# Mean over rows: the last group of rows loaded as 4, 4, 2 and 1 blocks, with five small stores

## The chip, the core and the metric

The kernel runs on one core of a Trainium2 chip. The metric is the device time of one execution in microseconds (us); before the change the median of three runs is 628.7 us (628.64 to 629.09). The profile's span, from the first to the last instruction, is 626.7 us in the profiled execution.

Engines go by these names: PE is TensorE (matmuls), with its weight loads as PEld; DVE is VectorE; ACT is ScalarE; POOL is GpSimd; SP is SyncE, which does no arithmetic here and issues transfers. SBUF is the on-chip memory of 128 partitions; PSUM is where TensorE's sums go.

## What is computed

```python
def setup_inputs():
    return {"x": np.random.randn(8192, 8192).astype(np.float32)}

def reference(x):
    return np.mean(x, axis=0)
```

x has 8192 rows and 8192 columns of 4 bytes, 268.4 MB, and each element is used once. The kernel takes the rows in 64 groups of 128, one row to a partition. Groups are added element by element into an accumulator `acc` of 128 x 8192, and at the end TensorE sums over the 128 partitions: a matmul with a stationary matrix filled with 1/8192 gives the mean of each column. The columns are counted in 16 blocks of F = 512.

## The kernel before

The buffers: four row buffers of 128 x 8192 that are loaded in turn, a fifth one `both` for the sum of a pair, and `acc`. PSUM holds three banks for blocks 0 to 11 and two ends for blocks 12 to 15.

```python
    F = 512
    W = F // 2
    WHOLE = 12
    G = M // P                     # 64 groups
    ...
    both = bufs[:, U - 2, :]
    acc = bufs[:, U - 1, :]
    ones = sb.tile([P, 32], f32, name="ones")
    ahead = sb.tile([P, 4 * F], f32, name="ahead")
    tail = sb.tile([P, W], f32, name="tail")
    ...
    banks = [psp.tile([P, F], f32, name=f"bank{b}") for b in range(3)]
    ends = [psp.tile([P, W], f32, name=f"end{e}") for e in range(2)]
```

All loads are issued by SyncE in program order. A load waits, through the buffer, for the VectorE add that last read it. VectorE's adds wait by way of a no-op on ScalarE or GpSimd, which gathers two waits into one. `landed` is a no-op on SyncE that waits for given transfers.

Three blocks of group 60 (`head`) and four blocks of group 63 (`ahead`) are loaded at the start, so that the last group has less to load. From group 6 to 53 the rows come in pairs: the two of a pair are added into `both`, and `both` into `acc`. From group 54 on they come one by one.

```python
    load(head[:], rows(G - 4)[:, :3 * F])
    first, second = load_rows(0, 0, 4), load_rows(4, 4, 2)
    load(ahead[:], rows(G - 1)[:, 8 * F:WHOLE * F])
    ...
    while g < G - 10:
        u = (g + 2) % 4
        dma = load_rows(g, u, 2)
        add(both, bufs[:, u, :], bufs[:, u + 1, :], [dma])
        add(acc, acc, both, [])
        g += 2

    while g < G - 4:
        row = bufs[:, (g + 2) % 4, :]
        add(acc, acc, row, [load(row, rows(g))])
        g += 1
    for lo, loaded in [(3, 3), (5, 0)]:               # groups 60 and 61
        row = bufs[:, (g + 2) % 4, :]
        dma = load(row[:, loaded * F:], rows(g)[:, loaded * F:])
        add(acc[:, lo * F:], acc[:, lo * F:], row[:, lo * F:], [dma])
        g += 1
    r61, r62, r63 = [bufs[:, (g + 1 + j) % 4, :] for j in range(3)]
    load(r62, rows(g))
    tc.keep_in_program_order(nc.gpsimd.tensor_add(
        out=acc[:, 13 * F:], in0=acc[:, 13 * F:], in1=r62[:, 13 * F:]))
    g += 1
    for lo, hi in [(0, 8), (12, 14), (14, 16)]:
        load(r63[:, lo * F:hi * F], rows(g)[:, lo * F:hi * F])
```

What VectorE and GpSimd do not add (parts of groups 60 to 63) goes to TensorE directly, in the order of a plan; the matmuls of one column add up in PSUM. A matmul uses a quarter of the array's columns (`tile_position`), so that four run side by side. Blocks 12 to 15 are cut in halves of 256 columns.

```python
    plan = [
        (ahead, 8, 12), (acc, 3, 5), (acc, 0, 3), (r61, 0, 5), (head, 0, 3),
        (acc, 5, 12), (r62, 0, 12), (r62, 12, 13), (acc, 12, 14), (acc, 14, 16),
        (r63, 0, 8), (r63, 12, 14), (r63, 14, 16),
    ]
    ...
        tc.keep_in_program_order(nc.tensor.matmul(
            out=dst[32 * q:32 * q + 32, :],
            lhsT=ones[:],
            rhs=cols,
            ...
            tile_position=(0, 32 * q),
        ))
```

Last come the copies out of PSUM and the stores. Four stores are made, two issued by ScalarE and two by SyncE.

```python
    copy(res[:, 2, :], banks[2][:])
    s2 = store(nc.scalar, out[8 * F:12 * F].rearrange("(q c) -> q c", q=4), res[0:P:32, 2, :],
               loads[-3])
    for b in range(2):
        copy(res[:, b, :], banks[b][:])
    copy(tails[0], ends[0][:])
    nc.vector.tensor_copy(out=tails[1], in_=ends[1][:])
    landed(*loads[-8:-6])
    landed(*loads[-6:-4])
    landed(*loads[-4:-2])
    landed(*joins.values())
    s01 = store(nc.sync, out[:8 * F].rearrange("(b q c) -> q b c", b=2, q=4), res[0:P:32, 0:2, :])
    s3 = store(nc.scalar, *end(0))
    store(nc.sync, *end(1))
    landed(loads[-2], s2)
    landed(loads[-1], adds[-1])
    landed(s01, s3)
    hold = tc.keep_in_program_order(nc.vector.nop()).ins
    tc.add_manual_dep(hold, s01.name, sync, reason="VectorE ends late")
```

## Time and profile before

| quantity | value |
|---|---|
| time, median of 3 | 628.7 us |
| span of the profiled execution | 626.7 us |
| VectorE busy | 526.1 us (84%), 60 instructions |
| TensorE busy | 17.6 us (3%), 124 matmuls |
| GpSimd busy | 4.0 us (1%) |
| ScalarE busy | 3.5 us (1%) |
| read from device memory | 268.44 MB, 428 GB/s over the span |
| first VectorE add starts | 43.77 us |
| GpSimd's add of 1536 columns | 615.74, for 3.47 us |
| last load's signal | 623.02 us |

The page of the profile cuts the span into 40 equal slices and gives, for each, the busy share of an engine in tenths, and of the 16 transfer engines as the row DMA. A group of instructions is one line: source line, engine, operation, output<-input with shapes, count, then total busy time and mean duration in ns, then the idle time ahead of it and what ended most of it. The chain of work that ended last is followed back from the last instruction; each piece gives its start, its length and what it was. In a timeline, SPq and ACTq are the queues on which SyncE and ScalarE issue transfers; the time of such an issue is not the time of the transfer.

### The profile page before, as it was taken

What the parts mean: (1) busy time and instruction counts of PE and PEld (TensorE: products, weight loads), DVE (VectorE), ACT (ScalarE), POOL (GpSimd) and SP (SyncE); (2) the same over time, 40 slices, a digit from 0 to 9 for tenths busy, and PEclk for the clock granted to TensorE, in tenths of its full rate; (3) what the DMA queues carried; (4) which work ended last, traced back from release to release, by engine and by line L of the source; (5) the groups of instructions that cost most, each with busy time, mean ns of one, the idle gap of its engine ahead of it and who ended that gap; (6) DMA issues with size and microseconds to landing.
All of it is one profiled execution on the core that took longest, in us unless ns stands there. A gap on an engine that the chain in (4) does not pass through costs nothing.

```text
span 626.7 us, 475 instructions
## 1 busy us (share of the span) xinstructions
PE 17.6 (3%) x124; PEld 5.1 (1%) x124; DVE 526.1 (84%) x60; ACT 3.5 (1%) x6; POOL 4.0 (1%) x7
## 2 busy tenths in 40 slices
PE   0000100000000000000000000000000000000027
PEld 0000000000000000000000000000000000000002
DVE  0028999999888998888988889888898888999991
ACT  0000000000000000000000000000000000000001
POOL 0000000000000000000000000000000000000002
PEclk9999999999999999999999999999999999999999
DMA  9999999999999999999999999999999999999997
GB/s 385 468 402 409 461 443 427 410 460 406 464 402 468 402 468 402 468 402 468 402 468 402 468 402 468 402 460 410 443 427 414 456 402 435 435 435 435 420 433 305
DMA packets 5926, 268.50 MB, mean 428 GB/s; under 512 B 656, under 2 KB 664, under 8 KB 1060
## 3 DMA queue, kind: packets, MB, share of 16 engines
q1 hardware_dynamic: 5908, 268.46, 99.2%
q8 instruction: 1, 0.02, 0.0%
q10 hardware_dynamic: 16, 0.01, 0.0%
q14 instruction: 1, 0.01, 0.0%
HBM read 268.44 MB, written 0.03 MB: 428 GB/s over the span
## 4 chain that ended last, share of the span: by engine, by line
DMA 56%; DVE 33%; another core or an unknown queue 10%; issue 0%; SPq 0%; PE 0%; ACTq 0%; POOLq 0%; POOL 0%
DMA bufs<-in_x_dram 56%; DVE bufs L95 33%; SPq L75 0%; PE end L169 0%; ACTq L98 0%; DVE tail L201 0%; POOLq L98 0%; POOL ready L62 0%; POOL ones L59 0%; POOLq L228 0%
## 5 line engine op out<-in xcount | busy, mean ns | idle before, releaser
L95 DVE TENSOR_TENSOR bufs<-bufs 128x8192 f32<-128x8192 f32 (+3 forms) x59 | 525.6, 8909 | 87.9 <-DMA bufs<-in_x_dram 43.8
L169 PE MATMUL bank<-bufs,ones 128*32 128x512 f32 x74 | 12.8, 709 | 540.4 <-DVE bufs L95 539.9
L201 DVE COPY tail<-end 128x256 f32<-128x256 f32 x1 | 0.4, 425 | 10.2 <-PE end L169 10.2
L169 PEld LDWEIGHTS bank<-bufs,ones 128*32 128x32 f32 x74 | 3.2, 120 | 549.5 <-DVE bufs L95 541.6
L136 POOL TENSOR_TENSOR bufs<-bufs 128x1536 f32<-128x1536 f32 x1 | 3.5, 3469 | 614.6 <-DMA bufs<-in_x_dram 614.6
L183 ACT COPY bufs<-bank 128x512 f32<-128x512 f32 x3 | 1.8, 586 | 619.2 <-PE bank L169 616.6
L169 PE MATMUL bank<-ahead,ones 128*32 128x512 f32 x8 | 1.9, 1058 | 65.7 <-DMA ahead<-in_x_dram 65.7
L169 PE MATMUL end<-bufs,ones 128*32 128x256 f32 x36 | 3.3, 384 | 0.1
L169 PE MATMUL bank<-head,ones 128*32 128x512 f32 x6 | 1.9, 600 | 0.0
L169 PEld LDWEIGHTS end<-bufs,ones 128*32 128x32 f32 x36 | 1.4, 109 | 2.4 <-DMA bufs<-in_x_dram 0.9
L116 ACT ACT_TABLE_LOAD x1 | 1.3, 1283 | 0.7 <-PEq L228 0.7
L169 PEld LDWEIGHTS bank<-ahead,ones 128*32 128x32 f32 x8 | 0.2, 140 | 65.6 <-issue 65.6
L183 ACT COPY bufs<-end 128x256 f32<-128x256 f32 x1 | 0.4, 378 | 0.0
L169 PEld LDWEIGHTS bank<-head,ones 128*32 128x32 f32 x6 | 0.4, 108 | 0.6 <-issue 0.6
L116 ACT COPY warm<-ones 128x32 f32<-128x32 f32 x1 | 0.2, 218 | 0.0
L62 POOL TENSOR_TENSOR ready<-ones 128x1 f32<-128x1 f32 x1 | 0.2, 193 | 0.1
L59 POOL MEMSET ones<- 128x32 f32 x1 | 0.1, 125 | 0.3 <-POOLq L228 0.3
L228 POOL MEMSET const-bfloat16-1.0<- 128x1 bf16 x1 | 0.1, 101 | 0.0
L228 POOL MEMSET const-uint8-127<- 128x1 uint8 x1 | 0.1, 101 | 0.0
L228 POOL MEMSET const-float32-0.0<- 128x1 f32 x1 | 0.1, 99 | 0.2 <-issue 0.2
L228 POOL MEMSET const-float32-1.0<- 128x1 f32 x1 | 0.1, 99 | 0.0
## 6 DMA issues: line engine op xcount, KB each, us to landing
bufs<-in_x_dram SPq DMA_DIRECT2D x8, 4096.0 KB, 24.1
bufs<-in_x_dram SPq DMA_DIRECT2D x1, 3328.0 KB
bufs<-in_x_dram SPq DMA_DIRECT2D x1, 2048.0 KB, 20.2
ahead<-in_x_dram SPq DMA_DIRECT2D x1, 1024.0 KB
bufs<-in_x_dram SPq DMA_DIRECT2D x2, 512.0 KB, 21.5
head<-in_x_dram SPq DMA_DIRECT2D x1, 768.0 KB
bufs<-in_x_dram SPq DMA_DIRECT2D x26, 29.9
out_dram<-bufs ACTq DMA_DIRECT2D x1, 8.0 KB
```

The costliest lines, as they stand in the source:

```text
L59: nc.gpsimd.memset(ones[:], 1.0 / M)
L62: nc.gpsimd.tensor_add(out=ready[:], in0=ones[:, 0:1], in1=ones[:, 1:2]))
L95: ins = nc.vector.tensor_add(out=dst, in0=a, in1=b).ins
L116: tc.keep_in_program_order(nc.scalar.copy(out=warm[:], in_=ones[:]))
L136: tc.keep_in_program_order(nc.gpsimd.tensor_add(out=acc[:, 13 * F:], in0=acc[:, 13 * F:], in1=r62[:, 13 * F:]))
L169: tc.keep_in_program_order(nc.tensor.matmul(out=dst[32 * q:32 * q + 32, :], lhsT=ones[:], rhs=cols, start=all(d is not dst or k != q for d ...
L183: tc.keep_in_program_order(nc.scalar.copy(out=dst, in_=src))
L201: nc.vector.tensor_copy(out=tails[1], in_=ends[1][:])
L228: nc = _bacc.Bacc("TRN2", target_bir_lowering=False, num_devices=1)
```

## The change

The end is rearranged. Early on, two blocks of group 60 (14 and 15) and five of group 63 (9 to 13) are loaded instead of three and four, into one buffer `early`. The five of group 63 are added to `acc` by GpSimd in the middle of the run, behind groups 24 and 32, so that TensorE no longer takes any early block. VectorE adds blocks 0 to 13 of group 60 and blocks 3 to 13 of group 61; GpSimd adds blocks 14 and 15 of group 61 behind VectorE's last add, then 14 and 15, and 8, of group 62. TensorE takes three blocks of group 61 instead of five.

The late part of group 63 is 11 blocks instead of 12, as blocks 4 to 7, 0 to 3, 14 and 15, and 8. The five blocks 9 to 13 have all their sums before group 63 comes and are stored early as `wide`. Blocks 14 and 15 (`two`) are cut in quarters of 256 columns, block 8 (`last`) in quarters of 128, so that the last load is followed by four matmuls of 128 columns and a copy of 128 columns. There are five stores instead of four. It is meant to leave less to load, add, copy and store behind the last transfer.

```diff
--- before.py
+++ after.py
@@ -40,8 +40,7 @@
     M, N = x.shape
     P = nc.NUM_PARTITIONS
     F = 512
-    W = F // 2
-    WHOLE = 12
+    W = F // 4
     G = M // P
     U = 6
     sync = mybir.DependencyInfo(mybir.DependencyClass.Sync, mybir.DependencyReason.DATA)
@@ -53,15 +52,17 @@
     both = bufs[:, U - 2, :]
     acc = bufs[:, U - 1, :]
     ones = sb.tile([P, 32], f32, name="ones")
-    ahead = sb.tile([P, 4 * F], f32, name="ahead")
+    early = sb.tile([P, 7 * F], f32, name="early")
     tail = sb.tile([P, W], f32, name="tail")
     warm = sb.tile([P, 32], f32, name="warm")
     nc.gpsimd.memset(ones[:], 1.0 / M)
     ready = sb.tile([P, 1], f32, name="ready")
     tc.keep_in_program_order(
         nc.gpsimd.tensor_add(out=ready[:], in0=ones[:, 0:1], in1=ones[:, 1:2]))
-    banks = [psp.tile([P, F], f32, name=f"bank{b}") for b in range(3)]
-    ends = [psp.tile([P, W], f32, name=f"end{e}") for e in range(2)]
+    banks = [psp.tile([P, F], f32, name=f"bank{b}") for b in range(2)]
+    wide = psp.tile([P, 2 * F], f32, name="wide")
+    two = psp.tile([P, 2 * W], f32, name="two")
+    last = psp.tile([P, W], f32, name="last")
 
     loads = []
 
@@ -103,81 +104,97 @@
             tc.add_manual_dep(ins, nop.name, sync, reason="waits for both at once")
         elif adds:
             tc.declare_no_dep(ins, group="loads", reason="the add ahead waited")
+        tc.declare_no_dep(ins, group="early", reason="the no-op waited, or the add behind it")
         tc.add_to_no_dep_group("adds", ins)
         adds.append(ins)
 
-    head = sb.tile([P, 3 * F], f32, name="head")
-    load(head[:], rows(G - 4)[:, :3 * F])
+    load(early[:, 5 * F:], rows(G - 4)[:, 14 * F:])
     first, second = load_rows(0, 0, 4), load_rows(4, 4, 2)
-    load(ahead[:], rows(G - 1)[:, 8 * F:WHOLE * F])
+    load(early[:, :5 * F], rows(G - 1)[:, 9 * F:14 * F])
     add(bufs[:, 2:4, :], bufs[:, 2:4, :], bufs[:, 0:2, :], [first])
     add(bufs[:, 4:6, :], bufs[:, 4:6, :], bufs[:, 2:4, :], [second])
     add(acc, acc, both, [])
     tc.keep_in_program_order(nc.scalar.copy(out=warm[:], in_=ones[:]))
+    ahead = []
     g = 6
     while g < G - 10:
         u = (g + 2) % 4
         dma = load_rows(g, u, 2)
         add(both, bufs[:, u, :], bufs[:, u + 1, :], [dma])
-        add(acc, acc, both, [])
+        add(acc, acc, both, ahead)
+        ahead = []
+        if g in (24, 32):
+            lo, hi = (0, 4) if g == 24 else (4, 7)
+            cols = slice((9 + lo) * F, (9 + hi) * F)
+            ins = tc.keep_in_program_order(nc.gpsimd.tensor_add(
+                out=acc[:, cols], in0=acc[:, cols], in1=early[:, lo * F:hi * F])).ins
+            tc.add_to_no_dep_group("early", ins)
+            ahead = [ins]
         g += 2
 
     while g < G - 4:
         row = bufs[:, (g + 2) % 4, :]
         add(acc, acc, row, [load(row, rows(g))])
         g += 1
-    for lo, loaded in [(3, 3), (5, 0)]:
+    for lo, hi, loaded in [(0, 14, 14), (3, 14, 16)]:
         row = bufs[:, (g + 2) % 4, :]
-        dma = load(row[:, loaded * F:], rows(g)[:, loaded * F:])
-        add(acc[:, lo * F:], acc[:, lo * F:], row[:, lo * F:], [dma])
+        dma = load(row[:, :loaded * F], rows(g)[:, :loaded * F])
+        cols = slice(lo * F, hi * F)
+        add(acc[:, cols], acc[:, cols], row[:, cols], [dma])
         g += 1
     r61, r62, r63 = [bufs[:, (g + 1 + j) % 4, :] for j in range(3)]
     load(r62, rows(g))
-    tc.keep_in_program_order(nc.gpsimd.tensor_add(
-        out=acc[:, 13 * F:], in0=acc[:, 13 * F:], in1=r62[:, 13 * F:]))
+    for row, lo, hi in [(r61, 14, 16), (r62, 14, 16), (r62, 8, 9)]:
+        cols = slice(lo * F, hi * F)
+        ins = tc.keep_in_program_order(nc.gpsimd.tensor_add(
+            out=acc[:, cols], in0=acc[:, cols], in1=row[:, cols])).ins
+        if row is r61:
+            tc.add_manual_dep(ins, adds[-1].name, sync, reason="VectorE goes first")
     g += 1
-    for lo, hi in [(0, 8), (12, 14), (14, 16)]:
+    for lo, hi in [(4, 8), (0, 4), (14, 16), (8, 9)]:
         load(r63[:, lo * F:hi * F], rows(g)[:, lo * F:hi * F])
 
-    plan = [
-        (ahead, 8, 12),
-        (acc, 3, 5),
-        (acc, 0, 3),
-        (r61, 0, 5),
-        (head, 0, 3),
-        (acc, 5, 12),
-        (r62, 0, 12),
-        (r62, 12, 13),
-        (acc, 12, 14),
-        (acc, 14, 16),
-        (r63, 0, 8),
-        (r63, 12, 14),
-        (r63, 14, 16),
-    ]
     sums = []
-    for row, lo, hi in plan:
-        base = 8 * F if row is ahead else 0
-        if lo < WHOLE:
-            for i in range(lo, hi):
-                cols = row[:, i * F - base:(i + 1) * F - base]
-                sums.append((banks[i // 4], i % 4, cols))
-        else:
-            for c in range(lo * F, hi * F, W):
-                e, q = divmod(c // W - 2 * WHOLE, 4)
-                sums.append((ends[e], q, row[:, c:c + W]))
-    for n, (dst, q, cols) in enumerate(sums):
+
+    def blocks(row, lo, hi):
+        for i in range(lo, hi):
+            sums.append((banks[i // 4], i % 4, 0, row[:, i * F:(i + 1) * F]))
+
+    def spread(dst, row, lo, hi, part=slice(None)):
+        n = (hi - lo) * W
+        for c in range(0, n, F)[part]:
+            for q in range(4):
+                at = lo * F + q * n + c
+                sums.append((dst, q, c, row[:, at:at + min(F, n - c)]))
+
+    blocks(acc, 0, 3)
+    blocks(r61, 0, 3)
+    blocks(acc, 3, 8)
+    spread(wide, acc, 9, 14, slice(1))
+    blocks(r62, 0, 8)
+    spread(wide, r62, 9, 14, slice(1))
+    for row in (acc, r62):
+        spread(wide, row, 9, 14, slice(1, 2))
+    blocks(r63, 4, 8)
+    spread(two, acc, 14, 16)
+    blocks(r63, 0, 4)
+    spread(last, acc, 8, 9)
+    spread(two, r63, 14, 16)
+    spread(last, r63, 8, 9)
+    for n, (dst, q, c, cols) in enumerate(sums):
         tc.keep_in_program_order(nc.tensor.matmul(
-            out=dst[32 * q:32 * q + 32, :],
+            out=dst[32 * q:32 * q + 32, c:c + cols.shape[1]],
             lhsT=ones[:],
             rhs=cols,
-            start=all(d is not dst or k != q for d, k, _ in sums[:n]),
-            stop=all(d is not dst or k != q for d, k, _ in sums[n + 1:]),
+            start=all((d is dst, k, at) != (True, q, c) for d, k, at, _ in sums[:n]),
+            stop=all((d is dst, k, at) != (True, q, c) for d, k, at, _ in sums[n + 1:]),
             tile_position=(0, 32 * q),
             skip_group_check=True,
         ))
 
-    res = both[:, :3 * F].rearrange("p (b c) -> p b c", b=3)
-    tails = [both[:, 3 * F:3 * F + W], tail[:]]
+    res = both[:, :2 * F].rearrange("p (b c) -> p b c", b=2)
+    res5 = both[:, 2 * F:2 * F + 5 * W]
+    res2 = both[:, 4 * F:4 * F + 2 * W]
 
     def copy(dst, src):
         tc.keep_in_program_order(nc.scalar.copy(out=dst, in_=src))
@@ -188,29 +205,29 @@
             tc.add_manual_dep(ins, o.name, sync, reason="follows that load")
         return ins
 
-    def end(e):
-        return (out[(WHOLE + 2 * e) * F:(WHOLE + 2 * e + 2) * F].rearrange("(q c) -> q c", q=4),
-                tails[e][0:P:32, :])
-
-    copy(res[:, 2, :], banks[2][:])
-    s2 = store(nc.scalar, out[8 * F:12 * F].rearrange("(q c) -> q c", q=4), res[0:P:32, 2, :],
-               loads[-3])
-    for b in range(2):
-        copy(res[:, b, :], banks[b][:])
-    copy(tails[0], ends[0][:])
-    nc.vector.tensor_copy(out=tails[1], in_=ends[1][:])
+    def part(lo, hi):
+        return out[lo * F:hi * F].rearrange("(q c) -> q c", q=4)
+
+    copy(res5, wide[:, :5 * W])
+    s5 = store(nc.scalar, part(9, 14), res5[0:P:32, :], loads[-4])
+    copy(res[:, 1, :], banks[1][:])
+    copy(res[:, 0, :], banks[0][:])
+    copy(res2, two[:])
+    nc.vector.tensor_copy(out=tail[:], in_=last[:])
     landed(*loads[-8:-6])
     landed(*loads[-6:-4])
     landed(*loads[-4:-2])
     landed(*joins.values())
-    s01 = store(nc.sync, out[:8 * F].rearrange("(b q c) -> q b c", b=2, q=4), res[0:P:32, 0:2, :])
-    s3 = store(nc.scalar, *end(0))
-    store(nc.sync, *end(1))
-    landed(loads[-2], s2)
+    s1 = store(nc.sync, part(4, 8), res[0:P:32, 1, :])
+    s0 = store(nc.sync, part(0, 4), res[0:P:32, 0, :])
+    s2 = store(nc.scalar, part(14, 16), res2[0:P:32, :])
+    store(nc.sync, part(8, 9), tail[0:P:32, :])
+    landed(loads[-2], s5)
     landed(loads[-1], adds[-1])
-    landed(s01, s3)
+    landed(s0, s1)
+    landed(s2)
     hold = tc.keep_in_program_order(nc.vector.nop()).ins
-    tc.add_manual_dep(hold, s01.name, sync, reason="VectorE ends late")
+    tc.add_manual_dep(hold, s0.name, sync, reason="VectorE ends late")
 
 
 # ---- launch: one core; inputs and outputs as the reference has them ----
```

## The prediction

> **What bounds the kernel now.** I read the page's transfer rows first.
>
> ```profile
> DMA  9999999999999999999999999999999999999997
> HBM read 268.44 MB, written 0.03 MB: 428 GB/s over the span
> ```
>
> All forty slices but the last have the transfer engines full, and 268.44 MB is all of x, read once. The change reads the same bytes, so only two things can move the time: a hole in the transfers, or the stretch after the last of them. The timeline of two periods in the middle tells how far a hole is.
>
> ```profile
> 201.06 17.42 DVE L95 TENSOR_TENSOR bufs<-bufs 128x8192 f32<-128x8192 f32 x2 [1.93 <-ACTq L98]
> ...
> 220.42 17.42 DVE L95 TENSOR_TENSOR bufs<-bufs 128x8192 f32<-128x8192 f32 x2 [1.94 <-POOLq L98]
> ```
>
> A pair of groups (8.39 MB) takes 220.42 - 201.06 = 19.36 us, 433 GB/s. VectorE adds for 17.42 of them and is idle for 1.93. A narrower look finds the next load issued at 209.78, after the first add of the pair; the load already under way lands at about 220.4. So a load is issued 10.6 us before the queue would run dry: the distance to a hole.
>
> Then the end, in the chain of work that ended last:
>
> ```profile
> 601.09 21.93 DMA bufs<-in_x_dram
> 623.02 0.04 issue
> 623.06 0.68 PE end L169 x8
> 623.75 0.03 issue
> 623.77 0.42 DVE tail L201
> ```
>
> The last load's signal comes at 623.02; eight matmuls of 256 columns, one copy of 256 columns and a store follow. After that the span runs to 626.7. SyncE's own waits by line show what closes it:
>
> ```profile
> L70 SPq EVENT_SEMAPHORE  x7: 17/28/28, 620.5 to 625.4; - x7
> ```
>
> ```profile
> L239 SPq EVENT_SEMAPHORE  x4: 17/17/28, 625.7 to 626.6; - x4
> ```
>
> The first is SyncE's last wait in the kernel, for the ACT store and the large SyncE store (625.4); the second begins when the tail store is in (625.7), and the closing exchange between engines takes the last 1.0 us. The tail store was issued at 624.22, so it needed about 1.5 us; it is last by only 0.3 us. That slim lead decides how much of a gain remains.
>
> [...]
>
> [...] before, GpSimd's one long add starts at 615.74 and VectorE's last add ends at about 613.5. The change does put GpSimd adds beside VectorE adds.
>
> [...] from 607.47 the weight loads are 0.86 us apart, from 612.60 some 0.43 us, so it took 5.1 us. The change alters when TensorE is busy.
>
> **The change part by part.** The rows for durations, with shapes kept apart:
>
> ```profile
> L95 DVE TENSOR_TENSOR bufs<-bufs 128x8192 f32<-128x8192 f32 x55 | 478.1, 8692 | 41.8 <-ACTq L98 28.9 <-POOLq L98 11.0
> ...
> L95 DVE TENSOR_TENSOR bufs<-bufs 128x5632 f32<-128x5632 f32 x1 | 6.0, 6027 | 0.1
> L136 POOL TENSOR_TENSOR bufs<-bufs 128x1536 f32<-128x1536 f32 x1 | 3.5, 3469 | 614.6 <-DMA bufs<-in_x_dram 614.6
> L169 PE MATMUL end<-bufs,ones 128*32 128x256 f32 x36 | 3.3, 384 | 0.1
> ...
> L183 ACT COPY bufs<-end 128x256 f32<-128x256 f32 x1 | 0.4, 378 | 0.0
> ...
> L62 POOL TENSOR_TENSOR ready<-ones 128x1 f32<-128x1 f32 x1 | 0.2, 193 | 0.1
> ```
>
> VectorE: (8692 - 6027) / 2560 = 1.041 ns a column. GpSimd: (3469 - 193) / 1535 = 2.134 ns a column, so 4.56 us for 2048, 2.38 for 1024 and 1.29 for 512 columns. These are estimates from the rows.
>
> 1. Early loads: 2 + 5 blocks instead of 3 + 4. Same seven blocks, no time. The first add starts about 0.26 MB / 430 GB/s = 0.6 us sooner, which the stream swallows.
>
> 2. GpSimd adds in groups 24 and 32, 4.56 and 3.47 us. Each can start when VectorE finishes the accumulating add, where VectorE is idle for 1.9 us. [...] VectorE's next add starts up to 4.56 - 1.93 = 2.6 us late, and so does the next load's issue. Of the 10.6 us to a hole, 8 remain. VectorE wins back 1.9 us per pair and is level again two pairs later. On the path to the end: 0.
>
> 3. Group 60 is loaded with 14 blocks, VectorE's add of it is 7168 columns: 6.03 + 1536 x 1.041 ns = 7.63 us instead of 7.09. VectorE's last add ends at about 614.0 instead of 613.5. TensorE has work for that but no deadline until the end: 0.
>
> 4. Group 62 has landed when 11 blocks of group 63 remain instead of 12: 2.88 MB / 431 GB/s = 6.7 us before 623.02, at 616.3. GpSimd then does 1024 columns of group 61 (614.0 to 616.4), 1024 of group 62 (to 618.8) and 512 (to 620.1). The first two are needed in TensorE's order after the matmuls of group 63's first four blocks, which land at 623.02 - 1.84 MB / 425 GB/s = 618.7; the third only after its next four, which land at 621.2. Both are in time, the second with over 1 us to spare.
>
> 5. The last four loads end at about 618.7, 621.2, 622.4 and 623.0. Block 0 to 3: four matmuls of 512 columns, about 0.6 us, copied by 622.4, its store issued on SyncE by 623.0. Blocks 14 and 15: 0.38 us of matmul, 0.38 us of copy on ScalarE, done by 623.2; ACT store issued from 623.25 instead of 623.48.
>
> 6. The tail itself. After the last signal there remain four matmuls of 128 columns, one in each column quarter, instead of eight of 256 in two rounds. One 512-column matmul is about 0.60 us and one of 256 is 0.38, so 128 columns are about 0.28: done at 623.35 instead of 623.74, 0.4 us less. The copy loses 128 columns at 1.041 ns: 0.29 instead of 0.42 us, 0.13 less. Store issued at 623.7 instead of 624.22. Sum: 0.5 us sooner, and if it still needs 1.5 us, it has landed at 625.2 instead of 625.7.
>
> 7. But the ACT store, last but one before, gains only 623.48 - 623.25 = 0.2 us: it lands near 625.2 too, where SyncE waits for it ahead of the closing wait, with some 0.1 us between. So of 0.5 us I count 0.4.
>
> Sum: 628.7 - 0.4 = 628.3 us.
>
> **The rivals.** *The other stores set the end.* Five small stores instead of four, two of them on SyncE ahead of the tail. For it: the tail leads by only 0.3 us now, and each issue costs SyncE 0.56 to 0.70 us. Against it: the large SyncE store is split, and its later half can go out a good 0.5 us before the tail. If it is so, the gain is 0.1 to 0.2 us: 628.5 to 628.6.
>
> *VectorE and GpSimd collide in the middle.* For it: two adds of 4.6 and 3.5 us[...]. Against it: 10.6 us to a hole against 4.6 us at most. If the stream did break, each collision would cost its excess, 1 to 3 us: 630 to 633.
>
> *The clock.* TensorE now works in two short bursts, at about 608 (six matmuls) and from 614.0, and could still be at half clock for group 63. Against it: from 614.0 to about 618.5 there is no gap. At half clock the last round takes about 0.1 us more: 628.4.
>
> *The last loads run slower.* The last one has rows of 2 KB and there is one transfer more. The last 1 MB before, in rows of 4 KB, moved at 401 to 410 GB/s (two windows from 621 to 622) against 419 to 442 earlier. Another 5 to 10% on 0.8 MB would cost 0.1 to 0.2 us: 628.4 to 628.5.
>
> *A late GpSimd.* If its adds took 1.5 times as long, the 512-column sum would be done at 622 instead of 620.1, and TensorE would hold back all behind it: 0.5 us or more lost.
>
> **Range and chances.** The gain is a sum of two well-read terms (0.4 and 0.13) of which the closing wait, slow rows and clock can eat a part; the three times of before spread over 0.45 us. I say 628.3, with 627.9 to 628.7 holding it 8 times in 10. Both 2% limits are 12.6 us away: faster and slower have 1% each, slower only through a broken stream.
>
> **What would show it.** Right: the transfer row stays full, the last load's signal comes within 0.2 us of 623.0, four matmuls and a copy take about 0.3 and 0.29 us after it, and the tail store goes out near 623.7; VectorE shows a longer idle or a longer add once after groups 24 and 32, with the 19.36 us period kept. Wrong: the last signal moves later than 623.2 (transfers), VectorE's starts in the middle stay late over more than two pairs (collision), TensorE waits on GpSimd after 621 (late sum), or SyncE's last wait for stores ends at 625.4 or later (the other stores).

## The result and the profile after

| | before | after |
|---|---|---|
| time, median (lowest to highest), 5 runs each | 628.7 us (628.56 to 629.09) | 630.93 us (629.55 to 631.18) |
| ratio, 95% interval | | 1.0028 [1.0016, 1.004] |
| span of the profiled execution | 626.7 us | 629.1 us |
| first VectorE add starts | 43.77 us | 43.19 us |
| VectorE's last add ends | 613.5 us | 614.33 us |
| last load's signal | 623.02 us | 623.30 us |
| TensorE's last sum is done | 623.74 us | 625.82 us |
| tail store issued | 624.22 us | 626.64 us |

By the ratio of the runs the change makes the kernel slower by 0.28%; the medians differ by 2.2 us. 628.3 us had been predicted, and 628.7 was the upper end of the range. The busy row of the transfer engines stays full after the change:

```profile
DMA  9999999999999999999999999999999999999995
...
HBM read 268.44 MB, written 0.03 MB: 427 GB/s over the span
```

The last slice alone has a lower digit, since more of it lies behind the transfers. The chain of work that ended last (start, length, what) says what that is:

```profile
608.29 6.04 DVE bufs L96
...
614.37 2.77 PE bank L185 x9
...
625.58 0.23 PE last L185 x2
...
625.84 0.29 DVE tail L216
```

Before, the chain ran through the last load until 623.02. Now no load is in its end: from 614.37 to 625.82 it is TensorE without a pause. TensorE is 2.5 us behind the last load's signal when it is done, and the cause is visible in the spacing of its weight loads. The profile has two records for each of the program's matmuls: 118 for 59 after the change, and the 124 of the table for before are 62 matmuls. A block of 512 columns thus stands in it as two passes. Four passes run side by side in the four column quarters, and one round of four is 0.86 us apart from the next at half clock (after the change, from 615.22 to 616.08) and 0.43 us at full clock (from 620.04 to 620.47). That is 0.43 us a block at half clock, and 0.21 at full. The timeline of the weight loads before the change (start, busy time, what, and the idle time ahead in brackets):

```profile
607.47 0.21 PEld L169 LDWEIGHTS bank<-bufs,ones 128*32 128x32 f32 x8 [541.60 <-DVE bufs L95]
...
611.75 0.18 PEld L169 LDWEIGHTS bank<-bufs,ones 128*32 128x32 f32 x1 [0.68 <-issue]
612.60 0.12 PEld L169 LDWEIGHTS bank<-bufs,ones 128*32 128x32 f32 x1 [0.68 <-issue]
...
613.03 0.11 PEld L169 LDWEIGHTS bank<-head,ones 128*32 128x32 f32 x1 [0.29 <-issue]
```

and after the change:

```profile
608.30 0.22 PEld L185 LDWEIGHTS bank<-bufs,ones 128*32 128x32 f32 x6 [608.30 <-issue]
...
610.01 0.22 PEld L185 LDWEIGHTS bank<-bufs,ones 128*32 128x32 f32 x3 [0.64 <-issue]
614.37 0.20 PEld L185 LDWEIGHTS bank<-bufs,ones 128*32 128x32 f32 x8 [4.13 <-DVE bufs L96]
615.22 0.18 PEld L185 LDWEIGHTS bank<-bufs,ones 128*32 128x32 f32 x1 [0.66 <-issue]
...
619.49 0.20 PEld L185 LDWEIGHTS bank<-bufs,ones 128*32 128x32 f32 x4 [0.66 <-issue]
620.04 0.11 PEld L185 LDWEIGHTS bank<-bufs,ones 128*32 128x32 f32 x1 [0.35 <-issue]
...
620.47 0.11 PEld L185 LDWEIGHTS bank<-bufs,ones 128*32 128x32 f32 x1 [0.31 <-issue]
```

Before, thirteen blocks from 607.47 on bring TensorE to full clock at 612.60, ahead of the work that follows VectorE's last add. After, there are six blocks, 2.6 us of work at half clock, then a pause to 614.37, and the spacing of 0.86 us goes on until 619.49. The next round takes 0.55 us, so full clock comes within it. The trace also records the granted clock: full from 612.60 before the change, and from 619.72 after it.

What this costs can be estimated. From 614.37 on the plan holds 37 blocks; at 0.214 us a block they need 7.9 us, and to the last signal there are 8.9 us: one us of slack. The 5.4 us at half clock do the work of 2.7, so 2.7 us are lost, 1.7 more than the slack; the last sums need 0.5 us in any case. This estimate gives 2.2 us behind the signal, against 2.5 measured.

The backlog then delays the copies, which stand ahead of the stores. ScalarE's timeline after the change:

```profile
624.66 1.07 ACT L200 COPY bufs<-bank 128x512 f32<-128x512 f32 x2 [1.14 <-issue]
625.62 0.39 ACT L200 COPY bufs<-two 128x256 f32<-128x256 f32 x1
```

and SyncE's store issues:

```profile
625.27 1.28 SPq L203 DMA_DIRECT2D out_dram<-bufs  x2
626.64 0.50 SPq L203 DMA_DIRECT2D out_dram<-tail  x1
```

The tail's copy ends at 626.13, but SyncE is busy with the two stores until 626.55. The tail store leaves 0.5 us after its copy. From its issue to the end of the span it is 2.4 us, as before (624.22 to 626.7). So the whole 2.4 us in the spans lie ahead of that issue.

### The profile page after: what moved, and what is told of

It is laid out like the page before. It is cut to its first block, busy times and chain, and to the rows that moved or that the text cites. A ratio compares the mean times of both kernels' runs of the same rounds, so it can differ in the third digit from the quotient of the medians.

```text
span 629.1 us, 475 instructions
## 1 busy us (share of the span) xinstructions
PE 15.1 (2%) x118; PEld 5.1 (1%) x118; DVE 530.4 (84%) x60; ACT 3.5 (1%) x6; POOL 14.4 (2%) x11
## 4 chain that ended last, share of the span: by engine, by line
DMA 52%; DVE 36%; another core or an unknown queue 10%; PE 2%; issue 0%; ACTq 0%; POOLq 0%; POOL 0%
DMA bufs<-in_x_dram 52%; DVE bufs L96 36%; PE bank L185 1%; PE wide L185 0%; PE two L185 0%; ACTq L99 0%; PE last L185 0%; POOLq L99 0%; DVE tail L216 0%; POOL ready L61 0%; POOL ones L58 0%; POOLq L245 0%
## 5 line engine op out<-in xcount | busy, mean ns | idle before, releaser
L129 POOL TENSOR_TENSOR bufs<-bufs,early 128x2048 f32<-128x2048 f32 (+1 forms) x2 | 7.9, 3954 | 348.6 <-DVE bufs L96 348.6
L149 POOL TENSOR_TENSOR bufs<-bufs 128x1024 f32<-128x1024 f32 (+1 forms) x3 | 5.9, 1995 | 256.9 <-DVE bufs L96 256.8
L185 PE MATMUL wide<-bufs,ones 128*32 128x512 f32 (+1 forms) x32 | 5.9, 550 | 0.0
L185 PE MATMUL two<-bufs,ones 128*32 128x256 f32 x16 | 2.0, 379 | 0.0
L185 PEld LDWEIGHTS wide<-bufs,ones 128*32 128x32 f32 x32 | 1.9, 127 | 2.3 <-issue 1.6
L185 PE MATMUL last<-bufs,ones 128*32 128x128 f32 x16 | 1.4, 273 | 0.0
```

Of the source, the lines that this page charges most:

```text
L129: ins = tc.keep_in_program_order(nc.gpsimd.tensor_add(out=acc[:, cols], in0=acc[:, cols], in1=early[:, lo * F:hi * F])).ins
L149: ins = tc.keep_in_program_order(nc.gpsimd.tensor_add(out=acc[:, cols], in0=acc[:, cols], in1=row[:, cols])).ins
L185: tc.keep_in_program_order(nc.tensor.matmul(out=dst[32 * q:32 * q + 32, c:c + cols.shape[1]], lhsT=ones[:], rhs=cols, start=all((d is dst, ...
```

## First experiments: TensorE's clock, its work, and GpSimd in the middle

The theory: TensorE is late because its early work is too short to bring full clock. The rivals: it is late because the plan gives it less time behind VectorE's last add, or the GpSimd adds in the middle leave something late.

**a_fill8** puts eight matmuls behind the first six. They sum into a PSUM bank that nothing reads, so this is more work and no other result.

```diff
+    fill = psp.tile([P, F], f32, name="fill")
...
     blocks(r61, 0, 3)
+    for i in range(8):
+        sums.append((fill, i % 4, 0, r61[:, (i % 3) * F:(i % 3 + 1) * F]))
     blocks(acc, 3, 8)
```

> The changed kernel with eight extra matmuls of 512 columns between TensorE's first six and the rest; they read blocks of group 61 again and their sums go to a spare PSUM bank that nobody reads. Clock theory (TensorE is at half clock at 614.4 because it had nothing to do from 610.9 on, and then has 23 blocks of sums to make at 0.43 us each instead of 0.21): the extra matmuls run from about 610.9 to 614.3, the half clock ends by about 614, the 23 blocks are done near 619.5, TensorE waits for the last loads again, and the time falls to 628.3 to 628.8. Rival 1 (simply too many sums behind VectorE's last add): extra matmuls change nothing or add, 630 or more. Rival 2 (the last loads, GpSimd or the store issue on SyncE set the end): 629.5 to 631, as the changed kernel.

**a_fill8_early** puts the same eight in front of the first six, on blocks of another group, some 10 us earlier.

```diff
+    for i in range(8):
+        sums.append((fill, i % 4, 0, bufs[:, 2, i * F:(i + 1) * F]))
     blocks(acc, 0, 3)
```

> The changed kernel with the same eight extra matmuls, but ahead of TensorE's first six, on group 60 as soon as it is loaded (near 597 to 598), so that they leave the idle time from 610.9 to 614.4 as it is. Clock theory: no help, TensorE is at half clock from 614.4 for some 3 to 5.5 us as in the changed kernel, time 629.5 to 631.2. If any extra TensorE work, or only the changed layout of the program, did it: the time of the run with the extra matmuls in the gap, 628.3 to 628.8.

**a_five** gives TensorE five blocks of group 61 again, as before the change; VectorE's last add is two blocks shorter.

```diff
-    for lo, hi, loaded in [(0, 14, 14), (3, 14, 16)]:
+    for lo, hi, loaded in [(0, 14, 14), (5, 14, 16)]:
...
-    blocks(acc, 0, 3)
-    blocks(r61, 0, 3)
-    blocks(acc, 3, 8)
+    blocks(acc, 0, 5)
+    blocks(r61, 0, 5)
+    blocks(acc, 5, 8)
```

> The changed kernel, but TensorE takes five blocks of group 61 as before instead of three, and VectorE's last add is blocks 5 to 13 (4608 columns). Clock theory: TensorE has ten blocks (4.3 us at half clock) from 608.3 to 612.6, VectorE ends near 613.3, the idle time shrinks from 3.5 to 0.7 us and 21 blocks remain instead of 23: the half clock ends near 613 to 616, time 628.4 to 629.3. Rival (transfers, GpSimd, store issue): 629.5 to 631, as the changed kernel.

**a_nomid** leaves out the two GpSimd adds in groups 24 and 32, so the seven early blocks (five of group 63, two of group 60) are missing from the sums.

```diff
-            ins = tc.keep_in_program_order(nc.gpsimd.tensor_add(
-                out=acc[:, cols], in0=acc[:, cols], in1=early[:, lo * F:hi * F])).ins
-            tc.add_to_no_dep_group("early", ins)
-            ahead = [ins]
```

> The changed kernel without GpSimd's two adds in the middle, behind groups 24 and 32: the five early blocks of group 63 and the two of group 60 are left out of the sums. Clock theory and my prediction: these adds cost nothing on the path to the end, 629.5 to 631.2 as the changed kernel. Rival[...]: VectorE's add behind group 24 is 8.70 instead of 11.21 us and the last signal comes up to 2.5 us sooner, time 628 to 628.7.

| | median (lowest to highest), runs | ratio to before, 95% interval |
|---|---|---|
| a_fill8 | 630.38 us (628.48 to 630.61), 7 | 1.0024 [1.0013, 1.0034] |
| a_fill8_early | 630.0 us (629.5 to 631.33), 8 | 1.0024 [1.0013, 1.0034] |
| a_five | 628.52 us (628.25 to 630.51), 13 | 1.0001 [0.9992, 1.0009] |
| a_nomid | 630.1 us (628.32 to 631.2), 13 | 1.0023 [1.0015, 1.0032] |

a_five takes the loss away: TensorE is at full clock from 614.08 by the clock's record, 5.6 us sooner than after the change, and waits for the last load. Its weight loads, 0.86 us apart before that moment and 0.47 us in the round after it:

```profile
613.15 0.30 PEld L185 LDWEIGHTS bank<-bufs,ones 128*32 128x32 f32 x7 [0.55 <-DVE bufs L96]
614.01 0.21 PEld L185 LDWEIGHTS wide<-bufs,ones 128*32 128x32 f32 x4 [0.56 <-issue]
614.48 0.17 PEld L185 LDWEIGHTS wide<-bufs,ones 128*32 128x32 f32 x4 [0.26 <-issue]
...
623.26 0.16 PEld L185 LDWEIGHTS last<-bufs,ones 128*32 128x32 f32 x8 [0.51 <-DMA bufs<-in_x_dram]
```

It changes two things at once, though, since VectorE also ends sooner. a_fill8 changes the clock alone, and TensorE's weight loads there are as the theory has it, with full clock from about 612.8 and a wait at the end. But the time hardly moves:

```profile
624.64 0.16 PEld L188 LDWEIGHTS last<-bufs,ones 128*32 128x32 f32 x8 [2.00 <-DMA bufs<-in_x_dram]
```

TensorE is idle for 2.00 us, waiting for the last load. Of that load's 16 signals fifteen are in by 623.06, and the last comes at 624.60. Six of the seven runs lie at 630.27 to 630.61, the seventh at 628.48. So the clock had been mended, and another loss took its place. What I expected of this kernel failed in its number, and the cause was open here; the next section has it.

a_fill8_early is the control: the same eight matmuls, but with a pause behind them. TensorE is at half clock when VectorE's last add is done, as after the change, and it stays there until about 619.8:

```profile
614.01 0.20 PEld L188 LDWEIGHTS bank<-bufs,ones 128*32 128x32 f32 x8 [4.22 <-DVE bufs L97]
614.87 0.18 PEld L188 LDWEIGHTS bank<-bufs,ones 128*32 128x32 f32 x1 [0.66 <-issue]
```

It is not the number of matmuls that counts but their place. Its runs lie where those of the kernel after lie.

a_nomid clears the adds in the middle: without them the time is not the time of before. In its profile the clock went another way, which is worth seeing. After the pause TensorE starts at full clock, keeps it for some 1.2 us and then falls to half:

```profile
614.94 0.11 PEld L181 LDWEIGHTS bank<-bufs,ones 128*32 128x32 f32 x1 [0.30 <-issue]
...
616.63 0.17 PEld L181 LDWEIGHTS bank<-bufs,ones 128*32 128x32 f32 x3 [0.57 <-issue]
...
618.44 0.22 PEld L181 LDWEIGHTS bank<-bufs,ones 128*32 128x32 f32 x4 [0.64 <-issue]
```

By the clock's record it is full from 612.29, in the pause, half from 615.70, and full again from 619.11. So here the same six blocks did bring full clock, but late, and it was gone again 1.2 us after the pause. That the pause took it away is a reading. In these traces the granted clock follows the start of the work with a delay (3.9 us here, from 608.42 to 612.29; 5.1 us before the change), and where the steps fall varies. What comes of it is the same, too much half clock in the stretch that sets the end: TensorE has no pause there either.

The runs of a_nomid and of the kernel after spread over 1.6 to 2.9 us, far more than those of before (0.5), and the place of these steps goes with most of that. Each run has its mean granted clock on record. The mean counts all ahead of the first step as full, so a fall to half for 3.41 us after a first grant, as in a_nomid's profile, gives 0.997, and one rise alone, as in the profile after, gives 1.000. After the change, the two runs with 0.997 took 629.55 and 629.79 us and the three with 1.000 took 630.93 to 631.18. In a_nomid, nine with 0.997 took 629.67 to 630.39, three with 1.000 took 630.83 to 631.2, and the one with 0.999 took 628.32. Compared like with like, a_nomid is no faster than the kernel after.

## Second experiments: full clock with less work, and the late sixteenth signal

**a_fill2** brings the clock with two extra matmuls, both in one column quarter so that they run one behind the other. Nothing reads their sums.

```diff
+    fill = psp.tile([P, F], f32, name="fill")
...
     blocks(r61, 0, 3)
+    for i in range(2):
+        sums.append((fill, 0, 0, r61[:, i * F:(i + 1) * F]))
```

> The changed kernel with two extra matmuls of 512 columns, both in one column quarter, behind TensorE's first six: one alone takes as long as four side by side (1.7 us at half clock), so two fill 3.4 of the 3.5 idle us with 8 recorded weight loads and matmuls instead of the 32 of the eight-matmul run. Two causes (the half clock; and, once TensorE is in time, an instruction fetch of 16 KB that occupies one transfer engine for 1.1 us and makes the last load's signal late if it falls before the end of that load; taken to follow the position in TensorE's instructions): the half clock ends near 614, the fetch comes at 622.5 or later, and most runs take 628.3 to 628.8, a few 630.3 to 630.6. Clock alone: 628.3 to 628.8 in all. If extra TensorE work never helps: 630.0 to 630.6, as with eight.

**a_fill2_pad6** is a_fill2 with six more such matmuls at the start of the run, hundreds of us away from the end. It asks whether the number of TensorE instructions ahead matters for the late signal.

```diff
+    for i in range(6):
+        sums.append((fill, i % 4, 0, early[:, (5 + i % 2) * F:(6 + i % 2) * F]))
     blocks(acc, 0, 3)
```

> The same with six more extra matmuls at the very start of the run (on two blocks loaded by 4 us), so that TensorE's work at the end is the same and only 24 more recorded instructions lie ahead of it. Two causes: the instruction fetch comes earlier, before the last load is done, one of its 16 signals is 1 to 2 us late, and most runs take 630.0 to 630.8. Clock alone: no difference to the run with two, 628.3 to 628.8.

**a_five_hold** is a_five with VectorE's last no-op waiting for another store. It asks whether a fetch of 8 KB (so the packets on transfer queues of the kind "instruction" are called here) that follows VectorE's end is what delays SyncE's last step, of which the next section tells.

```diff
-    tc.add_manual_dep(hold, s0.name, sync, reason="VectorE ends late")
+    tc.add_manual_dep(hold, s2.name, sync, reason="VectorE ends late")
```

> The run with five blocks of group 61 on TensorE, with VectorE's closing no-op waiting for the store of blocks 14 and 15 (in at 625.3) instead of the store of blocks 0 to 3 (in at 624.7). In that run an 8 KB instruction fetch started 1.13 us behind this no-op's end and SyncE's second closing step waited for it (626.39 instead of about 626.1). Theory: the fetch moves behind the closing steps, 0.2 to 0.3 us less: 628.2 to 628.4. If the fetch has nothing to do with the no-op: 628.5 as that run.

**b_noearly** goes from the other side: the kernel before, without the thirteen early matmuls. Their sums are left out, so TensorE has less to do.

```diff
-        (acc, 3, 5),
-        (acc, 0, 3),
-        (r61, 0, 5),
-        (head, 0, 3),
```

> The kernel before with 13 of TensorE's matmuls left out of the sums: the five early blocks of acc, five of group 61 and three of group 60, all that it did between 607.5 and 613.5. Clock theory: TensorE then starts on its 24 blocks at 613.5 at half clock, works through them until 621 or later instead of 619, ends up to 1 us late although it has less to do: 628.7 to 629.6. If only the amount of work counts: 628.4 to 628.6, the same as before or faster.

| | median (lowest to highest), runs | ratio to before, 95% interval |
|---|---|---|
| a_fill2 | 628.53 us (628.28 to 628.73), 13 | 0.9999 [0.9991, 1.0007] |
| a_fill2_pad6 | 630.44 us (628.34 to 630.92), 21 | 1.0022 [1.0015, 1.0029] |
| a_five_hold | 628.72 us (628.31 to 630.88), 21 | 1.0005 [0.9999, 1.0012] |
| b_noearly | 629.42 us (628.78 to 630.89), 21 | 1.0016 [1.0009, 1.0022] |

a_fill2 settles the clock. It adds two matmuls to the kernel after, changes nothing on VectorE, GpSimd or in the transfers, and its median is 2.4 us lower:

```profile
610.51 0.18 PEld L188 LDWEIGHTS fill<-bufs,ones 128*32 128x32 f32 x1 [0.63 <-issue]
611.24 0.11 PEld L188 LDWEIGHTS fill<-bufs,ones 128*32 128x32 f32 x1 [0.55 <-issue]
...
614.01 0.16 PEld L188 LDWEIGHTS bank<-bufs,ones 128*32 128x32 f32 x8 [1.80 <-DVE bufs L97]
614.47 0.11 PEld L188 LDWEIGHTS bank<-bufs,ones 128*32 128x32 f32 x1 [0.30 <-issue]
...
623.00 0.16 PEld L188 LDWEIGHTS last<-bufs,ones 128*32 128x32 f32 x8 [0.47 <-DMA bufs<-in_x_dram]
```

Full clock comes at 611.1, survives the 1.80 us of idle time, and TensorE waits 0.47 us for the last load instead of being 2.5 us late.

b_noearly shows the same in the kernel before, though less purely. With thirteen matmuls less TensorE starts at half clock at 613.67, has full clock from 618.05, and is done with the last sum at 624.23 instead of 623.74; the tail store is issued 0.6 us later, and the profiled span is 627.4 instead of 626.7 us. Less work, and a later end. But the median time rises by 0.8 us and the median span by only 0.3 (627.0 against 626.7), so most of that rise lies outside the span, and the runs do not say where. A fetch, told of next, comes at 629.68 in that profile, behind the span's end.

The late sixteenth signal has a trace of its own. Each of these kernels shows, beside the loads, one packet of 16,384 bytes on a queue of the kind "instruction". The last load's signals, from the trace, in us:

```
                16 KB packet starts, takes    15th signal   16th signal
a_fill2         622.20   1.09                 622.96        622.96
a_five          622.51   1.03                 623.21        623.22
a_fill8         622.43   1.09                 623.06        624.60
a_fill2_pad6    622.06   1.05                 622.87        624.28
```

In a_fill2_pad6 all packets of the last load have started by 622.4 except two of 2 KB, which start at 623.09 and 623.31; the instruction packet ended at 623.11. In a_fill8 one starts at 623.51, just as that packet ends at 623.52. This fits one transfer engine that served the fetch first and its share of the last load after it; a packet's record does not name its engine. In a_fill2 and a_five, packets of the same size and length (1.09 and 1.03 us) come with no late signal. They may have fallen to an engine that was done with its share; neither reading is shown. In the two where the last signal is late, TensorE waits 1.9 to 2.0 us.

How often this happens depends on the kernel. Counting the runs above 630 us, it is none of 13 in a_fill2, 1 of 13 in a_five, 2 of 21 in a_five_hold, 6 of 7 in a_fill8 and 15 of 21 in a_fill2_pad6. t_best, told of below, has the TensorE program of a_fill2 and 1 of 13, so a_fill2's own rate need not be zero. Of the single late runs only the time is known; that they have the same cause is assumed. Six matmuls at the far end of the run moved it from none to 15 of 21. That speaks for TensorE's stream of instructions, but the packet's record does not say whose instructions it holds, and the packet came only 0.14 us earlier with six matmuls more. Whose they are, and what decides which transfer engine it hits, stays open.

In a_five_hold the fetch of 8 KB moved from 625.87 to 626.35, and SyncE's last drain (one of the DRAIN instructions with which the engines close the program) came at 626.4 as in a_five. The fetch is not what delays it; that theory fell.

## Third experiments: SyncE's closing step, and a faster version

With TensorE in time, a_fill2 has the tail store out at 623.82, 0.4 us sooner than before the change, but its span ends only 0.2 us sooner. In the closing exchange SyncE's last drain comes at 626.20 there, against 626.25 before. The trace has 77 SyncE instructions before the change, 80 after it and 81 in a_fill2; the texts put down before the runs count one more in each (78, 81 and 82). Two kernels test whether that number matters.

**b_sp82** is the kernel before with eight more calls of `landed`, for loads that have long landed. In its trace SyncE has four waits more than before, 81 instructions in all.

```diff
+    for k in range(9, 17):
+        landed(loads[-k])
     landed(*loads[-8:-6])
```

> The kernel before with four more SyncE instructions: no-ops that wait for loads long landed, at a place where SyncE is idle for some 19 us. Theory: SyncE has 82 instructions, its second closing step comes 0.3 to 0.5 us late, 628.9 to 629.1. Rival: no difference, 628.4 to 628.7.

**t_best** is a_fill2 with SyncE's stores of the two banks joined into one and its waits merged, 77 SyncE instructions again. It is also the try for a version that beats both.

```diff
-    landed(*loads[-6:-4])
...
-    s1 = store(nc.sync, part(4, 8), res[0:P:32, 1, :])
-    s0 = store(nc.sync, part(0, 4), res[0:P:32, 0, :])
+    s0 = store(nc.sync, out[:8 * F].rearrange("(b q c) -> q b c", b=2, q=4), res[0:P:32, 0:2, :])
...
-    landed(loads[-1], adds[-1])
-    landed(s0, s1)
-    landed(s2)
+    landed(loads[-1])
+    landed(s0, s2)
```

> The run with two extra matmuls, with fewer instructions on SyncE: the stores of blocks 0 to 3 and 4 to 7 are one again, and three waits of no-ops that others cover are merged or dropped, so that SyncE has 78 instructions as before the change, instead of 82. In the runs with 81 or 82, SyncE's second closing step comes 0.37 to 0.48 us after it could; in the kernel before (78) it does not. Theory[...]: the closing is short again and the tail's gain shows, 628.1 to 628.3. Rival (the late step belongs to the five stores or to the fetch behind VectorE's no-op): 628.4 to 628.7, as the run with two.

**t_five** is a_five with the same edit on SyncE.

> The run with five blocks of group 61 on TensorE (no extra matmuls), with the same reduction to 78 SyncE instructions. Theory: 0.3 us faster than that run, 628.1 to 628.4 in most runs, with a few at 630.2 to 630.6 where the 16 KB fetch falls into the last load. Rival: 628.5 to 628.7.

| | median (lowest to highest), runs | ratio to before, 95% interval |
|---|---|---|
| b_sp82 | 628.86 us (628.66 to 629.5), 13 | 1.0004 [0.9996, 1.0012] |
| t_best | 628.33 us (628.07 to 630.8), 13 | 0.9999 [0.999, 1.0007] |
| t_five | 628.48 us (628.27 to 630.64), 13 | 1.0003 [0.9995, 1.0011] |

The last two of SyncE's drains in the closing exchange, here called first and second, from the traces in us:

```
             SyncE instructions   first    second   it takes
before       77                   626.00   626.25   0.01
b_sp82       81                   626.06   626.68   0.12
a_fill2      81                   625.57   626.20   0.11
t_best       77                   625.62   625.86   0.01
```

In the four traces the step from first to second drain is 0.24 to 0.25 us with 77 instructions and 0.62 to 0.64 us with 81. The other traces agree: 0.24 us in the kernel after, a_fill8_early and a_nomid with 80 and in b_noearly, t_five and t_split with 77; 0.62 to 0.79 us in a_five, a_five_hold, a_fill8, a_fill2_pad6 and a_split with 81. So the kernel after, which the text on t_best counts among those with the late step (its 81 are 80 here), does not have it. In time the step is little: b_sp82's median is 0.22 us above that of before on the same chip (628.64), just under what the theory said, its span 0.3, and the interval of the ratio holds 1. The late drain is shown by the traces; its mechanism is not.

t_best has both mended, and the tail's gain shows: span 626.3 us instead of 626.7, and twelve of thirteen runs at 628.07 to 628.76. Its median is 0.3 us below that of before, but one run at 630.8 and an interval that holds 1 leave it without a proof. t_five shows less: its span is 626.4 us in the profile against a_five's 626.7, but its median is only 0.04 us below that of a_five, not 0.3, and two of thirteen runs are late. No version here clearly beats the kernel before.

## Last experiment: the clock kept busy by a split add

**a_split** keeps TensorE's share at three blocks and cuts VectorE's last add in two instead, so that TensorE gets blocks 3 to 7 some 3 us sooner and has no long pause. **t_split** adds the SyncE edit of t_best.

```diff
-    for lo, hi, loaded in [(0, 14, 14), (3, 14, 16)]:
+    for lo, hi, loaded in [(0, 14, 14), (3, 8, 16)]:
...
+    add(acc[:, 8 * F:14 * F], acc[:, 8 * F:14 * F], row[:, 8 * F:14 * F], [])
+    tc.add_manual_dep(adds[-1], adds[-2].name, sync, reason="that one waited for the load")
```

> The changed kernel with VectorE's add of group 61 as two, blocks 3 to 7 and then 8 to 13, so that TensorE gets five blocks of acc at 611.1 instead of 614.4: nothing is left out and nothing is done twice. Clock theory: TensorE's first six blocks end at 610.9, five more last to 613 at half clock, full clock by 614 to 615; 18 blocks remain, done by 620.5; TensorE has 8 fewer recorded instructions than in the run with two extra matmuls, so the 16 KB fetch comes at or behind the end of the last load and no run is 2 us late: 628.4 to 628.7 in all. Rival to the fetch (late last signals come by chance in any of these programs): about one run in ten at 630.2 or more. Rival to the clock: 629.5 or more.

> The same with 78 instead of 82 SyncE instructions (one store for blocks 0 to 7, merged waits). Both theories together: 0.2 to 0.4 us less than with 82, 628.1 to 628.4, and no run at 630. Rivals: as the run with 82, or one run in ten at 630.2 or more.

| | median (lowest to highest), runs | ratio to before, 95% interval |
|---|---|---|
| a_split | 629.38 us (628.94 to 629.68), 21 | 1.0012 [1.0005, 1.0019] |
| t_split | 629.15 us (628.76 to 629.39), 13 | 1.0007 [0.9999, 1.0015] |

The clock does as meant, full from 613.28 in a_split and from 611.83 in t_split, and TensorE waits for the last load; no run is above 630. Yet both miss the times that were expected and are slower than a_fill2 and t_best by 0.8 us. The last load's signal comes at 624.22 in a_split:

```profile
624.26 0.16 PEld L187 LDWEIGHTS last<-bufs,ones 128*32 128x32 f32 x8 [0.48 <-DMA bufs<-in_x_dram]
```

Fifteen of the 16 signals are in by 623.15, and the same holds for every load since 492 us. VectorE's timeline in a_split, and then in the kernel after, shows the moment:

```profile
472.12 17.42 DVE L96 TENSOR_TENSOR bufs<-bufs 128x8192 f32<-128x8192 f32 x2 [1.94 <-ACTq L99]
492.44 8.69 DVE L96 TENSOR_TENSOR bufs<-bufs 128x8192 f32<-128x8192 f32 x1 [2.90 <-ACTq L99]
```

```profile
472.22 17.42 DVE L96 TENSOR_TENSOR bufs<-bufs 128x8192 f32<-128x8192 f32 x2 [1.92 <-ACTq L99]
491.57 8.69 DVE L96 TENSOR_TENSOR bufs<-bufs 128x8192 f32<-128x8192 f32 x1 [1.93 <-ACTq L99]
```

One wait of VectorE is 1 us longer. An instruction packet of 8,192 bytes stands ahead of it, and from then on the sixteenth signal of each load lags. From the traces, in us:

```
           8 KB packets after the start   lag of the 16th signal behind the 15th
after      628.87, 629.66                 never above 0.4
a_five     625.87, 627.01                 never above 0.4
a_split    486.11, 628.05                 1.05 to 1.13 from 492.4 to the end, none before
t_split    485.73, 628.76                 0.75 to 0.80 from 492.0 to the end, none before
```

VectorE has 68 instructions in the traces of the split kernels and 67 in the others. In these two kernels one 8 KB fetch falls into the stream, and only they show the lag, from the next landing on. That one transfer engine lost time there and, as the stream never pauses, stays behind to the end is a likely reading and not shown. The packet itself takes only 0.33 us in the record; why it leaves a lag of 0.75 to 1.1 us is not known.

## Why the prediction was wrong, step by step

**Step 1, early loads: right.** The first add starts 0.58 us sooner, 0.6 predicted, and the stream swallows it.

**Step 2, GpSimd in the middle: right in size and in effect.** The timeline of the kernel after at group 24:

```profile
276.85 4.49 POOL L129 TENSOR_TENSOR bufs<-bufs,early 128x2048 f32<-128x2048 f32 x1 [275.72 <-DVE bufs L96]
278.69 28.76 DVE L96 TENSOR_TENSOR bufs<-bufs 128x8192 f32<-128x8192 f32 x3 [1.92 <-ACTq L99]
```

GpSimd takes 4.49 us (4.56 predicted) and runs until 281.34. VectorE's next three adds follow each other in 28.76 us without the usual pause of 1.9 us: the first takes 11.21 instead of 8.70 us, and the 2.5 us too much are nearly the 2.65 us from 278.69 to GpSimd's end. In a_nomid, without that GpSimd add, the first two of these adds take 17.42 us, with the pause of 1.93 us behind them. So VectorE is held for nearly all of the overlap here; in the prediction, that GpSimd could hold it at all was an assumption. The transfers do not notice (the page's DMA row stays at 9 in every slice but the last), and a_nomid shows that leaving the adds out brings nothing back. The rival of a collision falls.

**Step 3, here it failed.** VectorE's times were right: 7.62 and 6.03 us, an end at 614.33 (614.0 predicted). The sentence behind them was wrong: "TensorE has work for that but no deadline until the end: 0". The later end and the smaller share of group 61 leave TensorE with 2.6 us of work and then a pause, and it starts its main work at half clock. The deadline was there as a sum: 37 blocks in 8.9 us, which full clock keeps and half clock does not.

**Step 4, GpSimd's late adds: right.** (By its own rate 512 columns are 1.28 us, not 1.29, which changes nothing.) They run from 614.45 to 620.47, predicted 614.0 to 620.1, and TensorE, late itself, does not wait for them.

**Step 5, the last loads: landing right, sums too small.** The four loads land at 618.9, 621.4, 622.7 and 623.3, 0.2 to 0.3 us later than predicted. The matmuls were sized as "about 0.6 us" for four of 512 columns. They are two rounds of passes, which with their end take 1.07 us even at full clock (a_fill2, from 621.09). I took the duration of one record for that of one matmul.

**Steps 6 and 7, the tail: right in kind, smaller, and only where TensorE is in time.** In a_fill2 the last signal is at 622.96 and the tail store goes out 0.86 us later, against 1.20 us before the change. That is 0.34 us of gain instead of 0.5: the last sums take 0.47 us, where I said 0.28. Here too I took records for matmuls: the "eight of 256 in two rounds" of before are four matmuls with two records each, so that the sums after the last signal went from two rounds of passes to two shorter ones, not from two to one. The copy takes 0.29 us as predicted. In a_fill2 the late SyncE drain takes about as much; in t_best the 0.34 us remain. Step 7's ACT store did not become the last wait.

**The rival "The clock" was the right one, sized wrongly.** It had the burst at 608 and the half clock. I set it at 0.1 us, on the ground that "from 614.0 to about 618.5 there is no gap", and looked only at the last round. The numbers for a better answer were there: 5.1 us from start to full clock in the kernel before, and six blocks of early work, where thirteen had taken from 607.47 to 613.5, or 0.46 us each: 2.8 us at most. How long the rise takes varies: from the start of the work to full clock it took 3.2 us in a_fill2, 5.1 before, 5.4 after and 5.9 in a_five. In the traces' records the stretches of one granted clock, but for the last, which the end of the record cuts off, are 3.41 us long in a_nomid (two of them), 10.24 us after the change and 13.65 us before it: one, three and four times 3.41. What sets the moment of a step is not shown. The six blocks alone brought no full clock in the profile after, and in a_nomid's only from 612.29 to 615.70. Half clock for 5.4 us from 614.37 loses 2.7 us; that product was never formed. Of the other rivals, stores that set the end cost 0.5 us in the profile after, only as a consequence of TensorE's backlog. Slow last loads cost about 0.2 us: from the landing of group 62 at 616.43 to the last signal it is 6.87 us, where 6.7 was predicted.

From the predicted issue of the tail store at 623.7 to the measured 626.64 it is 2.94 us: 0.28 from the last signal, 2.19 from TensorE (2.52 us behind the signal instead of 0.33) and about 0.5 from SyncE still busy with its two stores.

## What to carry to other kernels

When a change takes work from an engine that is not the bottleneck, work out what that engine's clock does in the stretch that sets the end: how long it is busy, how long it then pauses, and what the remaining work takes at half clock (here 0.43 us a block instead of 0.21). Compare that sum with the time to the last transfer, not only the last operation with the last signal. Where a short burst precedes a pause, reckon with either outcome: the same six blocks brought full clock in one profile (a_nomid, at 612.29) and not in the other (after, where it came at 619.72). At a tuned end of this kind, count instructions too: here a few more on TensorE, VectorE or SyncE went with a moved fetch or closing step that cost 0.4 to 2 us, as much as the change was to gain or more.

## What was not expected of the hardware

- Two matmuls that nobody reads, some 2 us of TensorE's time, make the kernel 2.4 us faster by the median (630.93 to 628.53), by keeping TensorE busy until the clock rises, at 611.1 in a_fill2.
- One instruction fetch of 16 KB, 1.03 to 1.09 us long, comes with one sixteenth of the last load 1.4 to 1.5 us late; with six matmuls more at the start of the run late runs went from none of 13 to 15 of 21.
- In the two kernels with one VectorE instruction more, a fetch of 8 KB came at 486 us, among the loads, and a lag of 0.75 to 1.1 us of one signal of every load stayed for the last 130 us.
- Four waits more on SyncE, all of them satisfied long before, put SyncE's second closing drain back by 0.4 us.
